# A transformer block on one core: another token order, other banks and tied products between output projection and up projection

## The chip, the core and the metric

The kernel runs on one core of one Trainium2 chip. The core has a matrix engine (TensorE, here PE, with its weight loads as PEld), a vector engine (DVE), a scalar engine (ACT), a general engine (POOL) and a queue that issues DMAs (SP). Each engine works through its own instructions in a fixed order and waits on semaphores for what the others deliver. [...] The metric is the device time of one execution in microseconds, lower is better.

## What is computed

One layer of a diffusion transformer: 1024 tokens of width 1024 on a 16 x 64 grid, 256 context tokens, 16 heads of 64 with a neighbourhood window of 8 x 16, and a gated feed-forward of width 2816.

```python
h  = modulate(rms_norm(x, norm1), sh1, sc1)        # sh, sc, g: adaLN of the condition c
hc = modulate(rms_norm(ctx, norm1), csh1, csc1)
q, k, v = heads(h @ w_q), heads(h @ w_k), heads(h @ w_v)     # q and k are RMS-normalised; kc, vc from hc
y  = neighbourhood_attention(q, k, v, kc, vc, rpb) @ w_o
x  = x + g1 * y
a, g = split(modulate(rms_norm(x, norm2), sh2, sc2) @ w_up)
out = x + g2 * ((a * gelu(dwconv3(g))) @ w_down)
```

All data are float32. The kernel multiplies in a faster reduced format (fp32r): each operand is split into a high part and a rest, and each product is three matmuls (high x high, high x rest, rest x high).

## The kernel before

The tokens are kept as eight tiles of 128 (NB = 8). The program runs in these stages:

1. adaLN of the attention branch and the first norm; tokens transposed and split.
2. Attention. For each of 8 pairs of heads the q, k and v projections (`qkv_gen`) are woven between the attention of the pair before. One step of attention (`stage_b`, `stage_c`, `stage_d`) handles one head and one tile of tokens: scores into the two banks with the tag "s", softmax on DVE, ACT and POOL, transposes of the probabilities through banks "tr" (three), the product with v into bank "po" (one). Two neighbouring tiles make a pair u, whose result goes to DRAM (`o_dram`, L456). In the last head the tiles come in the order LORD (L542).
3. Output projection (`wo_part`), in two halves over the heads. The first half (pairs of heads 0 to 3) runs beside the last heads' attention. The second half is the loop at L725: for each tile in the order TP it loads the heads' rows (L515), splits them (ACT L518, POOL L519), does 24 matmuls of 512 columns into two banks (L525 to L527) and adds them to the residual `x1[t]` (DVE L528). The banks are the two with tag "pq".
4. `h2_tile(t)` (L621): the residual goes to DRAM (L622); the second norm is a sum of squares on ACT (L155), a small DVE instruction (L156), a root on POOL (L157) and a scaling of all 1024 columns on DVE (L626). Eight PE transposes (L631) turn the tile, and four copies on DVE (L635) and four on ACT (L637) apply the modulation, writing back into `x1[t]`.
5. `combine(t)` (L695): the up projection uses seven products of half-size blocks in place of eight (Winograd's form). Its right-hand operands b1 to b7 are made of the token tiles: for a tile below 4 only b1 and b2 are split (ACT L646, then DVE L647, or POOL L647 for b3, b5 and b6); for tile 4 + m four sums with tile m (L710 to L713) and the splits of b3 to b7. Each of b1 and b2 is complete when tiles 0 to 3 are done; b3 to b7 need all eight. `combine` follows one tile late (LAG = 1).
6. Up projection. For each of 11 groups i of rows and its two parts (1 the gate, 0 the other factor) there are seven products in the order WORD, of 12 matmuls each (`up_mm`, L740). Part 1 sums in three banks "tr", part 0 in the two "pq" and in "po", and both use a half of "s" for the ops 7 and 4. The weights come by DMA (L667) into buffers `x1` that the token tiles have left; `raw_up` makes three sums of them (DVE L673 to L675) and `prep_up` splits an operand (ACT L687, POOL L688). The list `useq` sets the products' order in the program; operands are prepared up to six products ahead (UA = 6).
7. Convolution, gelu and gate of each group, and the down projection, also in seven products.

The program text gives a rank to each instruction. A planner then places them: it keeps a simulated clock for the engines and, when an engine is free, takes the ready instruction with the best rank, so the order on an engine can differ from the text. `tc.high_priority()` gives the instructions traced in its block a better rank. `tc.issue_after(ins)` adds an edge of order without a wait: what the block traces on the engine of `ins` is placed behind `ins` in that engine's queue. A buffer (`slot`, `xslot`, `ps.tile`) with a tag is given out again when the last reader of its former content is done.

Of the kernel before, what the change touches and what calls it, by code (L numbers as in the profile page):

```python
# [18 lines left out]
P = 128  # L19
# [23 lines left out]
TP = [0, 1, 4, 5, 2, 6, 3, 7]  # L43
LORD = [0, 1, 4, 5, 2, 3, 6, 7]
# [17 lines left out]
def block_kernel(ctx, tc, x, ctxt, cc, w_mod, b_col, b_row, n1, n2, w_qkv, gains, rpb_t, mask_i, mask_r, w_o,  # L62
# [96 lines left out]
    # adaLN of the attention branch, normalised and modulated tokens, transposed and split  # L159
# [112 lines left out]
    # attention, with the projections of the next pair of heads in between  # L272
# [185 lines left out]
    # adaLN of the rest, a little at a time  # L458
# [33 lines left out]
    # output projection: its first half runs beside the attention of the last heads  # L492
    xpool = ctx.enter_context(ExitStack())
    x1, wo, g1b, xsb = {}, [], [], []
# [18 lines left out]
    def wo_part(t, half):  # L513
# [6 lines left out]
        for hf in range(2):  # L520
            c = slice(hf * HALF, (hf + 1) * HALF)
            py = ps.tile([P, HALF], F32, tag="pq", bufs=2, name=f"py{half}_{t}_{hf}")
            for i in range(HP):
                wh, wl = wo[half * HP + i]
                PE.matmul(py, oh[:, i, :], wh[:, c], start=(i == 0), stop=False)  # L525
                PE.matmul(py, oh[:, i, :], wl[:, c], start=False, stop=False)  # L526
                PE.matmul(py, ol[:, i, :], wh[:, c], start=False, stop=(i == HP - 1))  # L527
# [14 lines left out]
    steps[-NB:] = [(NPAIR - 1, 1, t) for t in LORD]  # L542
# [62 lines left out]
    # rest of the output projection, second norm, operands of the Winograd form (seven products of halves  # L605
    # in place of eight) of the up projection: A is w_up^T in 2 x 2 blocks, B the tokens in 2 x 2 blocks
# [14 lines left out]
    def h2_tile(t):  # L621
# [4 lines left out]
        DVE.tensor_scalar(xn, x1[t], ss, None, ALU.mult)  # L626
        v = x1[t].rearrange("p (k n) -> p k n", n=P)
        for g in range(2):
            pt = ps.tile([P, 4, P], F32, tag="tr", bufs=3, name=f"pt2{t}_{g}")
            for k in range(4):  # L630
                PE.transpose(pt[:, k, :], xn[:, (4 * g + k) * P:(4 * g + k + 1) * P], ident)  # L631
# [17 lines left out]
    # up projection, gate with the token convolution; the gated rows and their sums go out for the down projection  # L649
# [4 lines left out]
    useq = [(0, 1, 1), (0, 1, 2), (0, 0, 1), (0, 0, 2)] + [(0, part, op) for part in (1, 0) for op in WORD[2:]]  # L654
# [23 lines left out]
    def prep_up(i, part, op):  # L678
        if (i, part) == (0, 1) and op in (1, 2):
# [15 lines left out]
    def combine(t):  # L695
# [3 lines left out]
        else:  # L699
# [18 lines left out]
            if t == 5:  # L718
                raw_up(0, 1)
                prep_up(0, 1, 1)  # L720
            if t == 6:
                prep_up(0, 1, 2)

    load_up(0, 0, 0)
    for n, t in enumerate(TP):  # L725
        wo_part(t, 1)
        vv[t] = h2_tile(t)
        if n >= LAG:
            combine(TP[n - LAG])
    for n in range(NB - LAG, NB):  # L730
        combine(TP[n])
# [82 lines left out]
    for k, (i, part, op) in enumerate(useq):  # L814
# [3 lines left out]
        if (i, part) not in gens:  # L818
            if part:
# [3 lines left out]
        next(gens[i, part])  # L823
# [156 lines left out]
```

## Time and profile before

| | |
|---|---|
| runs timed | 1492.29, 1489.33 and 1492.66 us |
| median of them | 1492.29 us |
| profiled execution, first to last instruction (span) | 1491.8 us |
| instructions | 22077 |
| mean granted clock of PE | 0.974 |
| PE busy | 1386.5 us |
| DVE busy | 1208.1 us |
| POOL busy | 805.7 us |
| ACT busy | 738.1 us |

The profiled execution is known by its span alone; it lies 0.5 us below the median of the timed runs. The profile's page has the busy time of each engine, a strip of 40 equal slices (each digit the busy share in tenths, PEclk the granted clock in tenths), and groups of instructions by line. The trace gives a timeline (start, duration, engine, line, operation, output <- inputs, shapes, how many merged, and in brackets the idle time before and what ended it), waits (who waited for whom: total, times, longest), and busy time by stretch. A line such as L740 is line 740 of the kernel before.

### The profile page before, as it was taken

The page shows a single profiled execution, that of the slowest core. Times are in us where ns is not written, and L with a number is a line of the kernel's source. Part 1 is how long each engine was busy: PE and PEld are TensorE (multiplying, and loading weights), DVE is VectorE, ACT ScalarE, POOL GpSimd, SP SyncE. Part 2 cuts the span into 40 slices and gives each one's busy share as a digit, 9 for nine tenths or more (in the row PEclk, how much of TensorE's full clock was granted, in tenths as well). Part 3 has the DMA queues.
Part 4 walks back from the last instruction along what each step waited for, and adds up shares of the span by engine and source line. Part 5 has one row for each costly group of instructions (what it writes and reads, how often), then busy time and mean ns, then how long its engine had stood idle before and what let it go on. Part 6 is the DMA issues. An engine that isn't in the chain of part 4 may idle for free.

```text
span 1491.8 us, 22077 instructions
## 1 busy us (share of the span) xinstructions
PE 1386.5 (93%) x7396; PEld 1200.0 (80%) x7396; DVE 1208.1 (81%) x2392; ACT 738.1 (49%) x1601; POOL 805.7 (54%) x672
## 2 busy tenths in 40 slices
PE   6689999999999999999996999999999987898998
PEld 2589889898989899888885777888888865686887
DVE  6778878888888878866589889788877779988884
ACT  6575645555565656645465434344343334244541
POOL 1455544545454546744368545555545568474872
PEclk9899999999999999999997999999999998899999
DMA  9612221313131202262132132233332347433343
GB/s 315 161 37 60 64 87 55 92 51 103 49 101 45 77 14 73 69 152 76 50 129 99 64 108 101 96 106 106 107 106 99 106 137 286 155 100 127 110 131 105
DMA packets 84827, 153.27 MB, mean 103 GB/s; under 512 B 9945, under 2 KB 49001, under 8 KB 84713
## 3 DMA queue, kind: packets, MB, share of 16 engines
q1 hardware_dynamic: 84712, 151.86, 32.7%
q8 instruction: 58, 0.95, 0.3%
q14 instruction: 57, 0.46, 0.1%
HBM read 119.05 MB, written 32.78 MB: 102 GB/s over the span
## 4 chain that ended last, share of the span: by engine, by line
PE 60%; DVE 20%; DMA 7%; POOL 5%; issue 4%; ACT 3%; SPq 0%; DVEq 0%; POOLq 0%; ACTq 0%
PE pg L740 8%; PE pa L740 7%; PE sw L740 6%; PE pq L301 5%; PE pq L303 5%; PE pq L305 5%; DMA mr<-in_w_mod_dram 2%; DVE y L787 2%; DVE p L410 2%; POOL u L688 2%; PE s L398 2%; PE po L448 2%; PE po L449 2%; PE py L525 2%; PE py L526 2%
## 5 line engine op out<-in xcount | busy, mean ns | idle before, releaser
L688 POOL TENSOR_TENSOR u<-ur,u 128x512 fp32r<-128x512 f32 x154 | 231.9, 1519 | 176.8 <-ACT u L687 175.1
L417 POOL TENSOR_TENSOR p<-p,m 128x640 f32<-128x640 f32 (+1 forms) x128 | 157.3, 1230 | 157.0 <-DVE m L413 116.0
L301 PE MATMUL pq<-wh,hth 128*128 128x384 f32 (+1 forms) x640 | 219.7, 343 | 17.1 <-DVE kn L340 15.3
L305 PE MATMUL pq<-wh,htl 128*128 128x384 f32 (+1 forms) x640 | 215.2, 336 | 2.4 <-DVE htl L194 1.4
L303 PE MATMUL pq<-wl,hth 128*128 128x384 f32 (+1 forms) x640 | 215.0, 336 | 0.5 <-POOL wl L147 0.5
L687 ACT ACTIVATE u<-ur 128x512 fp32r<-128x512 f32 x154 | 93.9, 628 | 116.1 <-PE sw L740 45.4
L412 ACT ACTIVATE p<-p,m 128x640 f32<-128x640 f32 (+1 forms) x128 | 102.9, 804 | 84.3 <-DVE m L410 75.2
L301 PEld LDWEIGHTS pq<-wh,hth 128*128 128x128 f32 x640 | 124.8, 195 | 23.1 <-DVE kn L340 9.2
L325 POOL TENSOR_TENSOR qss<-qss,mhalf 128x4 f32<-128x4 f32 (+1 forms) x80 | 79.9, 999 | 97.0 <-DVE qss L324 82.8
L305 PEld LDWEIGHTS pq<-wh,htl 128*128 128x128 f32 x640 | 124.7, 195 | 3.2 <-DVE htl L194 3.2
L303 PEld LDWEIGHTS pq<-wl,hth 128*128 128x128 f32 x640 | 124.8, 195 | 1.6 <-issue 0.9
L787 DVE SCALAR_TENSOR_TENSOR y<-g,cw,y 128x896 f32<-128x896 f32 (+1 forms) x132 | 102.8, 842 | 19.2 <-ACT y L781 19.1
L449 PE MATMUL po<-pt,v 128*128 128x256 f32 x352 | 93.3, 293 | 2.1 <-DVE pt L437 2.1
L448 PE MATMUL po<-pt,v 128*128 128x256 f32 x352 | 93.8, 289 | 0.1
L895 ACT ACTIVATE db<-dr 128x512 fp32r<-128x512 f32 x77 | 47.4, 629 | 87.3 <-PE dx L911 55.7
L871 POOL TENSOR_TENSOR da<-da 128x512 fp32r<-128x512 f32 x44 | 74.9, 1725 | 27.4 <-ACT da L870 27.4
L896 POOL TENSOR_TENSOR db<-dr,db 128x512 fp32r<-128x512 f32 x44 | 64.9, 1494 | 45.6 <-ACT db L895 34.3
L410 DVE CUSTOM_DVE_ANT_0 p<-s,bias 128x640 f32<-128x640 f32 x96 | 78.3, 816 | 9.5 <-PE s L399 8.9
L436 ACT ACTIVATE pt<-pl 128x384 fp32r<-128x384 f32 (+1 forms) x128 | 58.0, 461 | 47.6 <-PE pl L429 46.6
L471 DVE SCALAR_TENSOR_TENSOR macc<-mr,cs,macc 128x256 f32<-128x256 f32 x112 | 65.0, 581 | 13.9 <-DMA mr<-in_w_mod_dram 13.0
L437 DVE TENSOR_TENSOR pt<-pl,pt 128x384 fp32r<-128x384 f32 (+1 forms) x128 | 65.4, 516 | 6.7 <-ACT pt L436 6.2
L449 PEld LDWEIGHTS po<-pt,v 128*128 128x128 f32 x352 | 66.6, 189 | 4.0 <-DVE pt L437 3.4
(258 smaller groups left out, 4184.3 us busy)
## 6 DMA issues: line engine op xcount, KB each, us to landing
ur<-in_w_up_dram SPq DMA_DIRECT2D x44, 512.0 KB
da<-act_dram SPq DMA_DIRECT2D x77, 256.0 KB
mr<-in_w_mod_dram SPq DMA_DIRECT2D x128, 128.0 KB
dr<-in_w_down_dram SPq DMA_DIRECT2D x22, 512.0 KB
wraw<-in_w_qkv_dram SPq DMA_DIRECT2D x56, 192.0 KB
mraw<-in_w_mod_dram SPq DMA_DIRECT2D x16, 512.0 KB
act_dram<-sa SPq DMA_DIRECT2D x11, 512.0 KB
act_dram<-y SPq DMA_DIRECT2D x11, 512.0 KB
```

Source lines behind the costliest of these rows:

```text
L301: PE.matmul(pq[:, c0:], hth[t][:, k, :], wh[:, c0:], start=(k == 0), stop=False)
L303: PE.matmul(pq[:, c0:], hth[t][:, k, :], wl[:, c0:], start=False, stop=False)
L305: PE.matmul(pq[:, c0:], htl[t][:, k, :], wh[:, c0:], start=False, stop=(k == KC - 1))
L410: DVE.tensor_tensor_reduce(out=dst, in0=src, in1=bb, scale=1.0, scalar=3e38, op0=ALU.add, op1=ALU.min, accum_out=m[:, 0:1])
L412: ACT.activation(w[:, :n], w[:, :n], AF.Exp, bias=m[:, 0:1], scale=-1.0, accum_out=m[:, 1:2])
L417: POOL.tensor_tensor(w[:, :n], w[:, :n], m[:, 2:3].broadcast_to([P, n]), ALU.mult)
L448: PE.matmul(po, v, th[:, j].rearrange("p a b -> p (a b)"), start=(m == 0), stop=False)
L449: PE.matmul(po, v, tl[:, j].rearrange("p a b -> p (a b)"), start=False, stop=(m == len(blks) - 1))
L687: ACT.activation(s[:, 0], r[op], AF.Copy)
L688: POOL.tensor_tensor(s[:, 1], r[op], f(s[:, 0]), ALU.subtract)
L740: PE.matmul(bank, a, b, start=(start and k == 0 and n == 0), stop=(k == 3 and n == 2), skip_group_check=True)
L787: DVE.scalar_tensor_tensor(o, i, w, o, ALU.mult, ALU.add)
```

## The change

It touches the last head, the second half of the output projection, and the first products of the up projection.

- The last head's attention runs its tiles in natural order (LORD is gone), and the tiles of the output projection come in the order 0, 1, 2, 4, 3, 5, 6, 7 in place of 0, 1, 4, 5, 2, 6, 3, 7.
- The second half of the projection sums in one tile `sy` with the tag "s" (the two score banks) in place of two with the tag "pq".
- For the tiles 6 and 7 (DIAG) the norm's factor is no longer applied to the 1024 columns. A diagonal matrix `dg` is made of it (identity times the factor, 128 columns, DVE), and the eight transposes become eight plain fp32 products of `x1[t]`'s blocks with `dg`.
- `useq` begins with part 0's products 1 and 2, then part 1's; before, it was the other way round. Part 0's two operands are prepared in `combine(4)`, from a load issued before the loop, into two buffers `x1`; part 1's raw weights are loaded and summed in `combine(6)`, where before this was `combine(5)` with operands prepared in `combine(5)` and `combine(6)`.
- The first four up products are traced under `issue_after` the last matmul of the output projection.
- `h2_tile(7)` and the last `combine(7)` are traced under high priority.

Comments that the change strips are left out.

```diff
--- before.py
+++ after.py
@@ -40,8 +40,8 @@
 WB = 21
 FT = -1
 WS = 512
-TP = [0, 1, 4, 5, 2, 6, 3, 7]
-LORD = [0, 1, 4, 5, 2, 3, 6, 7]
+TP = [0, 1, 2, 4, 3, 5, 6, 7]
+DIAG = (6, 7)
 GROUPS = [2, 3, 3, 3]
 LA, LB = 3, 2
 DA, DB = (2, 1, 7), (2, 1, 7)
@@ -489,9 +489,9 @@
                         DVE.scalar_tensor_tensor(dst, dst, 1.0, n2c[:, nk * hf:nk * (hf + 1)], ALU.add, ALU.mult)
                 yield
 
     xpool = ctx.enter_context(ExitStack())
-    x1, wo, g1b, xsb = {}, [], [], []
+    x1, wo, g1b, xsb, sy, last_wo = {}, [], [], [], [], []
     HP = NPAIR // 2
 
     def wo_prep(p):
@@ -519,12 +519,12 @@
         (POOL if half else DVE).tensor_tensor(ol, raw, f(oh), ALU.subtract)
         for hf in range(2):
             c = slice(hf * HALF, (hf + 1) * HALF)
-            py = ps.tile([P, HALF], F32, tag="pq", bufs=2, name=f"py{half}_{t}_{hf}")
+            py = sy[0][:, hf] if half else ps.tile([P, HALF], F32, tag="pq", bufs=2, name=f"py{half}_{t}_{hf}")
             for i in range(HP):
                 wh, wl = wo[half * HP + i]
                 PE.matmul(py, oh[:, i, :], wh[:, c], start=(i == 0), stop=False)
                 PE.matmul(py, oh[:, i, :], wl[:, c], start=False, stop=False)
-                PE.matmul(py, ol[:, i, :], wh[:, c], start=False, stop=(i == HP - 1))
+                last_wo[:] = [PE.matmul(py, ol[:, i, :], wh[:, c], start=False, stop=(i == HP - 1))]
             DVE.tensor_tensor(x1[t][:, c], py, x1[t][:, c], ALU.add)
 
     def wo_first():
@@ -539,7 +539,6 @@
             yield 20
 
     steps = [(p, h, t) for p in range(NPAIR) for h in range(2) for t in range(NB)]
-    steps[-NB:] = [(NPAIR - 1, 1, t) for t in LORD]
     useq_ = {}
     for p, h, t in steps:
         useq_.setdefault((p, h, t // 2), len(useq_) % 2)
@@ -623,12 +622,22 @@
         xn = slot("wx", f"xn{t}", F32)
         ss = const.tile([P, 1], F32, tag="ss", bufs=3, name=f"ss2{t}")
         norm_rows(x1[t], xn, ss)
-        DVE.tensor_scalar(xn, x1[t], ss, None, ALU.mult)
+        if t in DIAG:
+            src, dg = x1[t], usb.tile([P, P], F32, tag="dg", bufs=2, name=f"dg{t}")
+            DVE.tensor_scalar(dg, ident, ss, None, ALU.mult)
+        else:
+            src, dg = xn, None
+            DVE.tensor_scalar(xn, x1[t], ss, None, ALU.mult)
         v = x1[t].rearrange("p (k n) -> p k n", n=P)
         for g in range(2):
             pt = ps.tile([P, 4, P], F32, tag="tr", bufs=3, name=f"pt2{t}_{g}")
             for k in range(4):
-                PE.transpose(pt[:, k, :], xn[:, (4 * g + k) * P:(4 * g + k + 1) * P], ident)
+                c = slice((4 * g + k) * P, (4 * g + k + 1) * P)
+                if dg is None:
+                    PE.transpose(pt[:, k, :], src[:, c], ident)
+                else:
+                    PE.matmul(pt[:, k, :], src[:, c], dg, start=True, stop=True)
             for k in range(4):
                 kk = 4 * g + k
                 if g == 0:
@@ -646,12 +655,12 @@
             ACT.activation(h, r, AF.Copy)
             (POOL if op in HP_ else DVE).tensor_tensor(l, r, f(h), ALU.subtract)
 
     NP2 = NF // 2
     lo_, hi_ = slice(0, HALF), slice(HALF, SEQ)
     uraw, uop = {}, {}
     parts = [(i, part) for i in range(NP2) for part in (1, 0)]
-    useq = [(0, 1, 1), (0, 1, 2), (0, 0, 1), (0, 0, 2)] + [(0, part, op) for part in (1, 0) for op in WORD[2:]]
+    useq = [(0, 0, 1), (0, 0, 2), (0, 1, 1), (0, 1, 2)] + [(0, part, op) for part in (1, 0) for op in WORD[2:]]
     useq += [(i, part, op) for i, part in parts[2:] for op in WORD]
     cnt = [0]
 
@@ -676,7 +685,7 @@
         uraw[i, part] = {1: a11, 2: a12, 6: t2, 5: t1, 7: a21, 3: a12, 4: a22}
 
     def prep_up(i, part, op):
-        if (i, part) == (0, 1) and op in (1, 2):
+        if (i, part) == (0, 0) and op in (1, 2):
             s = xslot(f"u{i}_{part}_{op}", F32R)
         else:
             s = slot(("rh", "rl")[cnt[0] % 2], f"u{i}_{part}_{op}", shape=(P, 2, HALF))
@@ -715,20 +724,27 @@
             split_b(5, m, t1)
             split_b(6, m, t2)
             split_b(4, m, t4)
-            if t == 5:
+            if t == 4:
+                uraw[0, 0] = {op: load_up(0, 0, 0)[:, op - 1] for op in (1, 2)}
+                prep_up(0, 0, 1)
+                prep_up(0, 0, 2)
+            if t == 6:
                 raw_up(0, 1)
-                prep_up(0, 1, 1)
-            if t == 6:
-                prep_up(0, 1, 2)
 
     load_up(0, 0, 0)
+    sy.append(ps.tile([P, 2, HALF], F32, tag="s", bufs=1, name="sy"))
     for n, t in enumerate(TP):
         wo_part(t, 1)
-        vv[t] = h2_tile(t)
+        if t == TP[-1]:
+            with tc.high_priority():
+                vv[t] = h2_tile(t)
+        else:
+            vv[t] = h2_tile(t)
         if n >= LAG:
             combine(TP[n - LAG])
-    for n in range(NB - LAG, NB):
-        combine(TP[n])
+    with tc.high_priority():
+        for n in range(NB - LAG, NB):
+            combine(TP[n])
     raw_up(0, 0)
     tmp00 = xslot("tmp0_0")
 
@@ -816,11 +832,15 @@
             prep_up(*useq[nprep])
             nprep += 1
         if (i, part) not in gens:
-            if part:
+            if i not in g:
                 g[i] = [slot("wx", f"g{i}_{m}", F32) for m in range(2)]
                 y[i] = [slot("t4", f"y{i}_{m}", F32) for m in range(2)]
             gens[i, part] = up_part(i, part, g[i] if part else y[i])
-        next(gens[i, part])
+        if k < 4:
+            with tc.issue_after(last_wo[0].ins):
+                next(gens[i, part])
+        else:
+            next(gens[i, part])
         if op == WORD[-1]:
             if part:
                 for m in range(2):
```

## The prediction

> **What bounds the kernel now.** I read the page first, then busy time by stretch around the changed place, then what TensorE (PE) waited for there.
>
> ```profile
> span 1491.8 us, 22077 instructions
> PE 1386.5 (93%) x7396; PEld 1200.0 (80%) x7396; DVE 1208.1 (81%) x2392; ACT 738.1 (49%) x1601; POOL 805.7 (54%) x672
> PE   6689999999999999999996999999999987898998
> PEclk9899999999999999999997999999999998899999
> ```
>
> PE is busy 93% of the span, and the two strips have a hole in common: near the middle PE falls to 6 and the granted clock to 7. That slice is the passage from the output projection to the up projection, where all of the change lies.
>
> ```profile
> 731.50:786.60 55.10, 53.58 (x271) 44.36 (x271) 39.74 (x78) 33.34 (x84) 31.90 (x32) 1.00 0.37 123
> 786.60:827.00 40.40, 27.39 (x93) 20.87 (x94) 38.02 (x50) 20.83 (x51) 34.46 (x28) 0.75 0.24 78
> 860.00:1230.00 370.00, 364.96 (x1563) 292.70 (x1562) 304.77 (x356) 145.21 (x224) 197.24 (x131) 1.00 0.32 108
> ```
>
> The columns are length, then busy time of PE, PEld, DVE, ACT, POOL, the clock, the DMA share and GB/s. The projection's second half (first row) is PE-bound with DVE idle for 15.4 us. In the passage (second row) PE is idle for 40.40 - 27.39 = 13.0 us at a mean clock of 0.75, and DVE works 38.02 of 40.40 us: there DVE is the bound. The up projection (third row) is PE-bound again (364.96 of 370), so time won in the passage reaches the end.
>
> ```profile
> PE pt L631 <- DVE xn L626: 5.5, 2, 5.3
> PE pg L740 <- ACT b3h L646: 2.9, 1, 2.9
> PE sw L740 <- DVE b7l L647: 2.4, 1, 2.4
> PE pa L740 <- ACT b1h L646: 1.9, 1, 1.9
> PE py L525 <- DVE x L528: 1.2, 1, 1.2
> ```
>
> These are PE's waits from 722 to 840 us (total, times, longest). The longest of L631 (5.3) and the row of pa with b1h are both tile 3, last but one in the old order: the up products 1 and 2 need all of tiles 0 to 3, so none could start before tile 3 was normalised, transposed and split. The rows with b3h and b7l are tile 7's: its transposes held the banks, then its sums were late.
>
> ```profile
> 786.20 0.39 PE L527 MATMUL py<-woh,ohl 128*128 128x512 f32 x1
> 791.90 1.94 PE L631 MATMUL pt<-ident,xn 128*128 128x128 f32 x8 [5.32 <-DVE xn L626]
> 795.74 0.79 PE L740 MATMUL pa<-b1h,u 128*128 128x512 f32 x1 [1.90 <-ACT b1h L646]
> 794.31 0.14 DVE L156 TENSOR_SCALAR ss<-ss 128x1 f32<-128x1 f32 x1
> 795.45 5.52 POOL L688 TENSOR_TENSOR u<-ur,u 128x512 fp32r<-128x512 f32 x4
> 800.94 0.73 POOL L157 TENSOR_TENSOR ss<-ss,mhalf 128x1 f32<-128x1 f32 x1
> 801.70 1.77 DVE L626 TENSOR_SCALAR xn<-x,ss 128x1024 f32<-128x1024 f32 x1 [0.44 <-POOL ss L157]
> ```
>
> The last projection matmul starts at 786.20; the first up product runs at 795.74. Tile 7's root (L157) could have run after 794.45 and ran at 800.94, behind weight splits (L688) queued in front of it on POOL.
>
> **What is lost there.** Two windows of the up matmuls alone (L740; PE, PEld, clock, DMA share, GB/s), and one tile's eight transposes:
>
> ```profile
> 780.00:827.00 47.00, 24.82 (x77) 18.40 (x78) 0.78 0.23 79
> 827.00:840.00 13.00, 13.00 (x57) 10.52 (x56) 1.00 0.25 82
> 746.34 1.03 PE L631 MATMUL pt<-ident,xn 128*128 128x128 f32 x8
> ```
>
> At full pace a matmul takes 13.00 / 57 = 0.228 us. By 827 there were 77, worth 17.6 us, and 16 transposes, worth 2 x 1.03: 19.7 us of work in 40.4 us. So 20.7 us are lost, 13.0 idle and 7.7 to the slow clock. That is nearly all that the change can win.
>
> **The change, part by part.** *Token order 0, 1, 2, 4, 3, 5, 6, 7, with the last head in natural order.* Tile 3 moves from behind the end of the projection to the fifth place. Its eight transposes (1.03 us) go ahead on PE, and these DVE rows leave the passage:
>
> ```profile
> 790.00 1.76 DVE L626 TENSOR_SCALAR xn<-x,ss 128x1024 f32<-128x1024 f32 x1
> 793.03 1.37 DVE L635 TENSOR_SCALAR x<-pt,s,b 128x128 f32<-128x128 f32 x4 [0.67 <-PE pt L631]
> 795.72 2.69 DVE L647 TENSOR_TENSOR b1l<-x,b1h 128x256 fp32r<-128x256 f32 x2 [1.27 <-ACT b1h L646]
> 798.34 2.92 DVE L647 TENSOR_TENSOR b2l<-x,b2h 128x256 fp32r<-128x256 f32 x2
> 757.16 0.75 DVE L647 TENSOR_TENSOR b1l<-x,b1h 128x256 fp32r<-128x256 f32 x2
> ```
>
> Together 1.76 + 1.37 + 2.69 + 2.92 = 8.7 us. Earlier, where POOL is mostly idle, the same pair of splits took 0.75 (last row), so ahead they cost some 3.6 us, inside DVE's 15.4 idle. In exchange the heavy combines (tiles 4, 5) come one and two places later: that is a rival below. The heads' own order moves no work; the second half still needs the score banks read, and its last pair of tokens is still done last.
>
> *Score banks.* The second half's sums go to the two banks of the scores, two halves in turn as before with two buffers: cost nothing. It frees the banks of the up product's part 0, so that part 0's products 1 and 2 can be first. Their weights are split in the middle of the projection into freed x1 buffers: two POOL splits (1.65 us each in the passage, by the mean of the row below) leave it.
>
> ```profile
> L688 POOL TENSOR_TENSOR u<-ur,u 128x512 fp32r<-128x512 f32 x12 | 19.6, 1652 | 0.9 <-ACT u L687 0.5
> L675 DVE TENSOR_TENSOR ur<-ur,ur 128x512 f32<-128x512 f32 x3 | 2.6, 863 | 0.0
> ```
>
> *Four products tied behind the last matmul.* 4 x 12 x 0.228 = 10.9 us of PE work that needs only tiles 0 to 3. The tie itself is an order in PE's queue, no wait; queued behind it are only up products, which before ran later anyway.
>
> What this must cover is tile 7's chain. In an undisturbed tile the way from the projection's add to the end of the scaling is 752.90 to 756.38, 3.5 us:
>
> ```profile
> 752.90 0.69 DVE L528 TENSOR_TENSOR x<-py,x 128x512 f32<-128x512 f32 x1 [0.39 <-PE py L527]
> 755.63 0.75 DVE L626 TENSOR_SCALAR xn<-x,ss 128x1024 f32<-128x1024 f32 x1 [0.66 <-POOL ss L157]
> ```
>
> With some 2 us of transposes, 1.4 of copies out, an add and a split of op 5 (about 0.7 each on DVE and ACT, 1.65 on POOL) it is 10 to 11 us: just covered. If that cover is gone, PE stands idle as it does now.
>
> *Diagonal form for tiles 6 and 7.* The scaling of 1024 columns (0.75 undisturbed, 1.77 in the passage) becomes a 128-column one. No such row exists; its bounds are 0.14 (L156, one column) and 0.40 (L635, 128 columns out of PSUM). I take 0.3, saving 1.5 us a tile in the passage. PE multiplies in plain fp32 instead of transposing. The nearest fp32 product with a 128x128 stationary is L485, two calls, four records:
>
> ```profile
> 232.67 0.53 PEld L485 LDWEIGHTS pmc<-ones,macc 128*128 128x128 f32 x4
> ```
>
> The starts are (0.53 - 0.19) / 3 = 0.11 us apart (0.19: one load), two records a call, so eight calls take 16 x 0.11 to 0.12 = 1.9 us against 1.03. If they cost the same as transposes the extra is 0; if a record cost a full load of 0.19, 3.0 us and 2.0 extra. I take 0.9 extra for each tile.
>
> *Priority.* It moves tile 7's instructions ahead of weight splits on POOL, ACT, DVE and SP wherever the planner finds them ready. Worth up to 800.94 - 794.45 = 6.5 us, already within the 20.7. Tile 7's store of 512 KB (L622) moves too: SP stands at it until L528 ends, 0.7 us behind the projection, and the loads of weights queue behind it. The copies out overwrite the stored rows and wait for it: 3 to 4 us (256 KB took 2.95, quoted below) beside the chain's 3.5 and the 1.9 of products, so hidden; 1 us if it isn't.
>
> **The sum.** PE first. The projection ends at 786.6 - 1.2 (the wait for L528, bounds 0 and 1.2) + 1.0 (tile 3) + 0.9 (tile 6) = 787.3. From there 17.6 + 1.9 = 19.5 us without a stall: the state of 827 would be reached at 806.8, a gain of 20.2. Now DVE, the bound of the passage: 38.0 - 8.7 - 1.5 = 27.8 us of its work remain behind 787.3, which ends at 815.1, a gain of 11.9. But one of the three sets of L673 to L675 in that stretch is for the next part of weights (3 x 0.68 = 2.0), which PE doesn't need yet: 813.1, a gain of 13.9. I take this: PE won't run before DVE feeds it. Span 1491.8 - 13.9 = 1477.9; the runs' median lies 0.5 above the span, so 1478.4. Its own range is a gain of 9 to 20, 1472 to 1483.
>
> A short stall costs more than itself:
>
> ```profile
> 811.78 0.47 PE L740 MATMUL pg<-b2h,u 128*128 128x512 f32 x1 [2.93 <-ACT b3h L646]
> 811.80:816.40 4.60, 4.60 (x13) 0.63 0.64 216
> ```
>
> After 2.93 us of waiting the clock was 0.63 over 4.6 us, so 1.7 us more; the 6.3 us left between the two sums hold one such stall (4.6).
> [...]
>
> **Rivals.** *Weights of part 1 late (gain 4 to 9).* Part 0 now takes the x1 buffers that freed first, so part 1's loads wait for the combines of 5 and 6.
>
> ```profile
> 775.24 1.02 SPq L667 DMA_DIRECT2D ur<-in_w_up_dram  x2
> 808.10 8.94 SPq L667 DMA_DIRECT2D ur<-in_w_up_dram  x5
> 727.89 2.95 DMA oraw<-o_dram
> 782.59 1.85 POOL L647 TENSOR_TENSOR b6l<-x,b6h 128x256 fp32r<-128x256 f32 x2
> ```
>
> They went at 775.24; now at best after tile 5's last split (784.4 in the old order). With 3 to 4 us of landing (256 KB took 2.95), an ACT copy of 0.6 and a POOL split of 1.65 the operand is there at 791, before 787.3 + 5.5 + 1.9 = 794.7, when PE wants it. If the third buffer or the splits come 6 us later, PE waits 6 and slows for 1.7 to 3.4: of 13.9 remain 4 to 8; 1484 to 1488. For it: POOL's share in the passage, 34.46 of 40.40. Against: two more buffers free with the first two products.
>
> *The same, much later (gain near 0).* If the loads go at 808, as the second pair's did, the third product starts near 814, and 53 matmuls (12.1 us) at a clock first halved end at 828: 1491 to 1494.
>
> *Slower: the priority holds the queues.* DVE, ACT and POOL run in order. If the planner thinks tile 7's chain is ready earlier than it is, its instructions stand at the head of DVE while ready work waits behind. The price is DVE's idle time behind the projection's end: up to the whole chain, 11 us, and 5 more for the combine of tile 7 that hangs on it. DVE's 27.8 + 16 = 43.8 would end at 831, 4 later than before; 1492 to 1497. It decides from 40.4 + 786.6 - 787.3 - 27.8 = 11.9 us of such idle time. Against: now DVE idles only 2.4 us in that passage with the planner's own order.
>
> *The tie doesn't act so.* If tile 6's or 7's products stand in PE's order before the four, PE waits out the 3.5 us and half rate: 5 to 7 of the gain, 1483 to 1486; counted with the first rival.
>
> **Chances.** Forecast 0.60, more than 20 won 0.04, first and last rival 0.18, loads at 808 0.08, slower 0.10. A measurement of this kernel tells some 0.2% (3 us) from nothing, so faster 0.82, same 0.08, slower 0.10. The range holds the forecast and the partial gains: 1471 to 1489.
>
> **What would show it.** Right: four products start within 0.5 us of the last L527 and run some 11 us at full clock; no L631 wait above 2 us; DVE rows of tile 3 before the end of the projection; L157 of tile 7 within 1.5 us of its L156; DVE near 28 us from there to the 77th up matmul. Wrong: a PE gap over 3 us before the first product of part 1, loads of L667 behind 795, DVE idle above 8 us, or a projection that ends after 790.

## The result, and the profile after

The change makes the kernel slower: 1504.31 us, the median of four runs (1503.1 to 1504.95), against 1490.81 us, the median of four runs of the kernel before. The ratio is 1.0084, with a 95% interval of 1.0066 to 1.0102. Forecast was 1478.4. The profiled execution took 1503.1 us, with a span of 1501.3.

The page of the kernel after, its head and the two strips that were read before:

```profile
span 1501.3 us, 22103 instructions
PE 1386.5 (92%) x7412; PEld 1197.9 (80%) x7412; DVE 1215.6 (81%) x2392; ACT 739.9 (49%) x1601; POOL 802.0 (53%) x672
PE   6699999999999999989986999999999998798998
PEclk9899999999999999999998999999999999899999
```

PE is busy for the same 1386.5 us as before, so the longer span is idle time of PE. The hole in the middle is still there, at the same place and a little less deep at the clock (8 instead of 7).

The same stretches as before, in the kernel after: from the first matmul of the projection's second half to its end, from there to the 77th up matmul, and the up projection (length, busy PE, PEld, DVE, ACT, POOL, clock, DMA share, GB/s):

```profile
727.90:795.30 67.40, 60.01 (x288) 47.24 (x289) 41.81 (x89) 37.26 (x92) 30.64 (x31) 0.97 0.25 86
795.30:833.90 38.60, 23.63 (x94) 18.19 (x93) 37.18 (x38) 18.27 (x45) 36.99 (x31) 0.82 0.31 109
860.00:1230.00 370.00, 363.67 (x1552) 292.02 (x1551) 312.63 (x357) 145.27 (x221) 203.64 (x134) 0.99 0.30 104
```

The projection takes 67.4 us where it took 55.1, and PE idles 7.4 us of them (67.40 - 60.01; before 1.5). The passage takes 38.6 us where it took 40.4; 25.8 were forecast. DVE works 37.18 and POOL 36.99 of the 38.60 us, so between them these two fill the passage; before it was 38.02 and 34.46 of 40.40.

What PE waited for from 722 to 840 us in the kernel after:

```profile
PE sw L756 <- DVE b7l L656: 8.1, 1, 8.1
PE sy L525 <- DVE x L528: 6.4, 6, 2.0
PE pg L756 <- ACT x L646: 2.8, 1, 2.8
PE pa L756 <- ACT u L696: 2.2, 1, 2.2
```

The wait for tile 3's scaling (5.3 before) and that for b1h are gone. Two rows stand in their place: the longest wait is now for the low part of b7 (b7l), and the projection waits for its own copies out, L528, six times.

To compare all runs stage by stage, the times below count from the last score read-out of the attention, L410. Its rows in the kernel before and in the kernel after (shortest, median and longest in ns, first and last start):

```profile
L410 DVE DVE_READ_ACCUMULATOR2_ANT m<- x4: 83/84/85, 723.9 to 730.6; 128x1 f32 x4
```

```profile
L410 DVE DVE_READ_ACCUMULATOR2_ANT m<- x3: 82/82/83, 723.5 to 727.1; 128x1 f32 x3
```

So zero is 730.6 us in the one and 727.1 in the other. All kernels do the same work up to there, the last head's tiles in one of two orders. In the fourteen profiles zero lies between 724.9 and 731.1 us, with either order, so a difference there is not put down to an edit. One profiled execution stands for each kernel; the sums' distances from the 761.2 of the kernel before agree with those of the medians within 3 us. Marks are read off the timeline: the end of the last projection matmul, the start of the 77th and of the 1500th up matmul, the first down matmul, the end.

```
                   to the end of   to the    to the     to the first   to the   sum
                   the projection  77th up   1500th up  down matmul    end
before                  55.9         40.5      333.1        82.1        249.6   761.2
after                   68.2         38.6      334.8        82.6        250.0   774.2
e1_before_sy            73.3         31.0      334.7        83.0        248.9   770.9
e2_after_pq             56.0         43.7      335.3        87.9        250.4   773.3
e3_after_two            56.4         46.2      334.0        85.9        251.3   773.8
e4_after_order          69.0         32.6      335.2        87.6        249.5   773.9
e5_pq_order             58.3         39.9      335.8        83.1        250.5   767.6
e6_pq_nopri             55.9         43.8      335.5        85.9        250.5   771.6
e7_pq_nodiag            56.1         41.2      335.0        83.0        249.0   764.3
e8_pq_poolrelief        54.7         38.7      335.6        83.9        248.8   761.7
e9_pq_order_nodiag      58.4         37.6      335.2        81.3        250.2   762.7
e10_pq_order_nodiag_act 58.2         34.4      334.7        82.6        250.6   760.5
e11_before_diag         55.8         40.0      331.1        83.3        250.1   760.3
e12_pq_notie            55.8         43.9      335.2        87.7        249.0   771.6
```

The kernel after loses 12.3 us in the projection, wins 1.9 in the passage, and loses 1.7 by the 1500th up matmul and 0.9 behind it: 13.0. So the question is two questions: why did the projection become longer, and why did the passage not become shorter?

### The profile page after: what moved, and what is told of

It reads as the page before. It is cut to its first block, busy times and chain, and to the rows that moved or that the text cites. A ratio compares the mean times of both kernels' runs of the same rounds, so it can differ in the third digit from the quotient of the medians.

```text
span 1501.3 us, 22103 instructions
## 1 busy us (share of the span) xinstructions
PE 1386.5 (92%) x7412; PEld 1197.9 (80%) x7412; DVE 1215.6 (81%) x2392; ACT 739.9 (49%) x1601; POOL 802.0 (53%) x672
## 4 chain that ended last, share of the span: by engine, by line
PE 64%; DVE 18%; DMA 7%; issue 4%; ACT 3%; POOL 3%; SPq 1%; DVEq 0%; POOLq 0%; ACTq 0%
PE pg L756 8%; PE pa L756 8%; PE sw L756 6%; PE pq L301 5%; PE pq L303 5%; PE pq L305 5%; DMA mr<-in_w_mod_dram 2%; PE s L398 2%; PE dtr L929 2%; PE po L448 2%; PE po L449 2%; PE pl L429 2%; PE dtr L930 2%; PE dtr L931 2%; DVE y L803 1%
## 5 line engine op out<-in xcount | busy, mean ns | idle before, releaser
L325 POOL TENSOR_TENSOR qss<-qss,mhalf 128x4 f32<-128x4 f32 (+1 forms) x80 | 80.2, 1003 | 95.5 <-DVE qss L324 81.3
L803 DVE SCALAR_TENSOR_TENSOR y<-g,cw,y 128x112 f32<-128x112 f32 (+1 forms) x132 | 109.6, 897 | 21.4 <-ACT y L797 21.4
L891 POOL TENSOR_TENSOR da<-da 128x512 fp32r<-128x512 f32 x44 | 67.7, 1562 | 38.9 <-ACT da L890 38.9
L410 DVE CUSTOM_DVE_ANT_0 p<-s,bias 128x640 f32<-128x640 f32 x96 | 78.2, 815 | 9.0 <-PE s L399 8.2
L890 ACT ACTIVATE da<-da 128x512 fp32r<-128x512 f32 x77 | 47.9, 630 | 47.1 <-DMA da<-act_dram 46.1
```

What stands on the lines that cost most here:

```text
L325: POOL.tensor_tensor(ss[:, 4 - n:], ss[:, 4 - n:], mhalf[:, 4 - n:], ALU.pow)
L803: DVE.scalar_tensor_tensor(o, i, w, o, ALU.mult, ALU.add)
```

## The experiments

### First question: the projection

Theory: the two halves of the tile `sy` don't take turns as two buffers do; each half's first matmul waits for the copy out of the other half. Rivals: the new order of the tiles, or the diagonal products among the projection's matmuls. Two changes from the first half of a tile to its second in the kernel after (timeline; in brackets the idle time and what ended it):

```profile
745.12 0.39 PE L527 MATMUL sy<-woh,ohl 128*128 128x512 f32 x1
745.55 0.69 DVE L528 TENSOR_TENSOR x<-sy,x 128x512 f32<-128x512 f32 x1
746.39 0.47 PE L525 MATMUL sy<-woh,ohl 128*128 128x512 f32 x1 [0.88 <-DVE x L528]
...
771.64 1.76 DVE L720 TENSOR_TENSOR x<-x,x 128x512 f32<-128x512 f32 x1 [0.65 <-POOL x L719]
772.38 0.39 PE L527 MATMUL sy<-woh,ohl 128*128 128x512 f32 x1
773.33 0.74 DVE L656 TENSOR_TENSOR b7l<-x,b7h 128x256 fp32r<-128x256 f32 x2
774.00 0.68 DVE L528 TENSOR_TENSOR x<-sy,x 128x512 f32<-128x512 f32 x1
774.73 0.50 PE L525 MATMUL sy<-woh,ohl 128*128 128x512 f32 x1 [1.97 <-DVE x L528]
775.41 0.63 PE L527 MATMUL sy<-woh,ohl 128*128 128x512 f32 x1
775.83 0.63 PE L525 MATMUL sy<-woh,ohl 128*128 128x512 f32 x1
...
778.39 0.49 PE L525 MATMUL sy<-woh,ohl 128*128 128x512 f32 x1
```

The last matmul of one half ends at 745.51, DVE copies it out at once, and only then the next half's first matmul runs, though it writes another bank: 0.88 us of idle PE. In the second place DVE is busy with a combine (L720, L656) when the half is ready at 772.77, so the copy comes 1.2 us late and PE idles 1.97. Behind that gap eight matmuls start 0.43 us apart ((778.39 - 775.41) / 7) instead of 0.23. Between two tiles the change is covered by a tile's transposes (eight took 1.06 us at 749.64 us, and the next first matmul ran at 750.46 without a wait).

**e1_before_sy: only the sums in one tile.** The kernel before with this alone:

```diff
+    sy.append(ps.tile([P, 2, HALF], F32, tag="s", bufs=1, name="sy"))
...
-            py = ps.tile([P, HALF], F32, tag="pq", bufs=2, name=f"py{half}_{t}_{hf}")
+            py = sy[0][:, hf] if half else ps.tile([P, HALF], F32, tag="pq", bufs=2, name=f"py{half}_{t}_{hf}")
```

> The kernel before with one edit: the projection's second half sums in the two halves of one tile in the score banks; order, products and priority as before. Theory A (the two halves are waited for as one buffer: each half's first matmul waits for the copy-out of the other half): PE waits 6 to 8 us on L528 in that stage and the whole is 7 to 12 us slower than before, 1498 to 1503. Rival B (the waits come from a DVE that is late because the heavy combines moved; the banks cost nothing): no such waits, 1489 to 1493.

**e2_after_pq: the kernel after with the sums back in two tiles.** The same line the other way round.

> The changed kernel with the second half's sums back in two tiles of the old banks; everything else of the change stays. Theory A: the waits on L528 fall from 6.4 to below 2 us, the projection ends 8 to 12 us earlier after its first matmul, total 1493 to 1498. Rival B: the waits stay, total 1502 to 1506.

**e3_after_two: the first half in the score banks, the second in a "pq" tile.**

```diff
-            py = sy[0][:, hf] if half else ps.tile(...)
+            py = sy[0][:, hf] if half and hf == 0 else ps.tile(...)
```

> The changed kernel with only the first half of each token tile in the score banks and the second half in a tile of the old banks, so two halves are two tiles. Theory A: as with both in the old banks, 1493 to 1498. A third reading (the score banks themselves are slow to come free or to be read) would leave waits on every second half: 1498 to 1502. Rival B: 1502 to 1506.

**e4_after_order: the kernel after with the old order of tiles** in the projection and in the last head.

```diff
-TP = [0, 1, 2, 4, 3, 5, 6, 7]
+TP = [0, 1, 4, 5, 2, 6, 3, 7]
+LORD = [0, 1, 4, 5, 2, 3, 6, 7]
```

> The changed kernel with the token order and the last head's order of before; banks, tied products, diagonal form and priority as changed. Theory A: the waits on the one tile stay, about 6 us, and tile 3 is late again, so 1500 to 1508. Rival B (the late heavy combines are the cost): near before, 1489 to 1496.

Measured: e1 1503.05 us, ratio 1.0075 (1.0047 to 1.0103); e2 1503.43, 1.0085 (1.0057 to 1.0114); e3 1504.55, 1.0085 (1.0057 to 1.0113); e4 1505.99, 1.0098 (1.0063 to 1.0132). What PE waited for in e1 from 720 to 840 us:

```profile
PE sy L525 <- DVE x L528: 11.2, 7, 5.3
PE pt L631 <- DVE xn L626: 7.6, 3, 6.8
```

The one line of e1 brings the wait into the kernel before (11.2 us for L528, where 6 to 8 were expected) and lengthens its projection from 55.9 to 73.3. Two tiles instead of one, in e2 as in e3, where one of them even lies in a score bank, bring the kernel after back to 56.0 and 56.4. With the old order (e4) it stays at 69.0. So it is the one tile, not the banks and not the order, and the first theory holds for the projection. The trace puts the wait down to DVE's L528; no run tells whether the banks themselves would have needed it, or only the program's bookkeeping of the tile.

The times of e2 and e3 are another matter: 1493 to 1498 was expected, and they came out at 1503.43 and 1504.55, where the rival had them. e2 is no faster than the kernel after: the 12 us come back from the projection and are lost again behind it, 5.1 of them in the passage (38.6 to 43.7) and 5.3 on the way from the 1500th up matmul to the first down matmul.

### Second question: the passage

The passage of e2, in the same columns, and the first sums of the heavy combines on DVE in e2, and then in the kernel after:

```profile
782.50:826.20 43.70, 27.79 (x110) 20.94 (x109) 40.77 (x45) 21.81 (x54) 41.14 (x35) 0.77 0.32 109
785.87 0.69 DVE L720 TENSOR_TENSOR x<-x,x 128x512 f32<-128x512 f32 x1 [1.03 <-POOL x L719]
795.62 1.23 DVE L720 TENSOR_TENSOR w<-x,x 128x512 f32<-128x512 f32 x1
802.41 1.21 DVE L720 TENSOR_TENSOR x<-x,x 128x512 f32<-128x512 f32 x1
```

```profile
801.40 0.68 DVE L720 TENSOR_TENSOR x<-x,x 128x512 f32<-128x512 f32 x1
811.85 1.22 DVE L720 TENSOR_TENSOR w<-x,x 128x512 f32<-128x512 f32 x1
```

In e2 DVE and POOL both work for 41 of 43.7 us. Of the four heavy combines (tiles 4 to 7) three begin behind the end of the projection at 782.5; in the kernel after it is two, behind 795.3: its longer projection gave DVE and POOL time to start one more. That fits the 5.1 us that e2 loses in the passage; the 5.3 us before the first down matmul it doesn't explain.

Theory: the passage is bound by DVE and POOL, which carry the heavy combines and the weights at once. Rivals: the priority puts things in a bad order; the diagonal form costs more than its price; the tie doesn't cover tile 7. All four runs start from e2.

**e5_pq_order: the heavy tiles earlier.**

```diff
-TP = [0, 1, 2, 4, 3, 5, 6, 7]
+TP = [0, 1, 4, 5, 2, 3, 6, 7]
+LORD = [0, 1, 4, 5, 2, 3, 6, 7]
```

> The run with the old banks, and the tokens in the order 0, 1, 4, 5, 2, 3, 6, 7 (the last head as before): the heavy combines of 4 and 5 go early again, tile 3 still ends before the projection does. Theory C (the passage is long because the combines of 5, 6 and 7 all fall behind the projection's end): from the last scores to the 77th up matmul 84 to 90 us in place of 99.7, total 1486 to 1494. Rival D (sharing between DVE and POOL makes the same work take as long in any order): 96 to 100, total 1500 to 1504.

**e6_pq_nopri: without both priorities.**

```diff
-            with tc.high_priority():
-                vv[t] = h2_tile(t)
+            vv[t] = h2_tile(t)
...
-    with tc.high_priority():
-        for n in range(NB - LAG, NB):
-            combine(TP[n])
+    for n in range(NB - LAG, NB):
+        combine(TP[n])
```

> The run with the old banks, without both priorities. If the priority puts tile 7's combine ahead of tile 6's, which is needed as much: to the 77th up matmul 94 to 98 us in place of 99.7, 2 to 5 us faster. If the priority helps as meant: 102 to 106, slower by 2 to 6. If the planner's order is much the same: within 1.5.

**e7_pq_nodiag: tiles 6 and 7 scaled and transposed as before.**

```diff
-DIAG = (6, 7)
+DIAG = ()
```

> The run with the old banks, with the old scaling and transposes for tiles 6 and 7. If the diagonal form saves 1.5 us of DVE for each tile as predicted: to the 77th up matmul 102 to 103 us in place of 99.7. If its DVE instruction is stretched as much and its products hold PE: 98 to 100.

**e8_pq_poolrelief: less for POOL.** The subtraction that makes the low part of the first group's weights is left out; a copy on ACT fills the same buffer, and the products that use it stay.

```diff
-        POOL.tensor_tensor(s[:, 1], r[op], f(s[:, 0]), ALU.subtract)
+        if i == 0:
+            ACT.activation(s[:, 1], r[op], AF.Copy)
+        else:
+            POOL.tensor_tensor(s[:, 1], r[op], f(s[:, 0]), ALU.subtract)
```

> The run with the old banks; for the first group's 14 weight operands POOL doesn't subtract: the low part is a second copy of the full value on ACT, so the low part of these products is left out (replaced by another value). It takes about 21 us of POOL work out of the passage. Theory (POOL and DVE stretch each other and bound the passage together): DVE's 512-column sums fall from 1.2 to 1.75 us towards 0.68, to the 77th up matmul 80 to 87 us in place of 99.7. Rival (the combines' own order and chain bound it, whatever POOL does): 94 to 99.

Measured: e5 1496.39 us, ratio 1.0042 (1.0024 to 1.0059); e6 1504.98, 1.0094 (1.0072 to 1.0116); e7 1493.42, 1.0007 (0.9992 to 1.0021); e8 1492.67, 1.0015 (0.9997 to 1.0033). In the passage of e2, the work on the raw weights alone (tile `ur`; their sums on DVE, copies on ACT, subtractions on POOL, in this order); then in e8 the whole passage and the same part:

```profile
782.50:826.20 43.70, 14.46 (x11) 6.72 (x11) 17.25 (x12) 0.77 0.32 109
```

```profile
783.40:822.10 38.70, 24.84 (x109) 19.09 (x108) 30.55 (x48) 26.99 (x67) 26.99 (x23) 0.82 0.35 115
783.40:822.10 38.70, 11.79 (x14) 12.53 (x22) 0.00 (x0) 0.82 0.35 115
```

The priority changes nothing in the passage (43.8 against 43.7). The earlier heavy tiles take 3.8 us off the passage but add 2.3 to the projection. POOL's relief takes 5.0 us off the passage: DVE, whose own instructions were left alone, is busy 30.55 us instead of 40.77, and the weights' sums take 0.84 us each (11.79 / 14) instead of 1.31 (14.46 / 11). So POOL's work makes DVE's longer, and the theory holds in kind. In size it falls short: less than a third of POOL's 17.25 us comes back. PE's longest waits in e8 are for b7 (7.5 us for b7l, 5.2 for b7h), and no engine there is busy for more than 30.55 of the 38.70 us; this speaks for the rival, that the combines' own order and chain bound it. Without the diagonal form the passage is 2.5 us shorter.

The expectations named the 77th up matmul, 99.7 us behind zero in e2. It came at 98.2 in e5, where the rival had it (96 to 100) and not the theory (84 to 90); at 99.7 in e6, as for an order that stays the same; at 97.3 in e7, earlier than both expectations had it (98 to 100 and 102 to 103); and at 93.4 in e8, between the theory's 80 to 87 and the rival's 94 to 99 and nearer the rival's.

In e5, e7 and e8 much of the gain in time lies elsewhere: e7 is 10.0 us faster than e2, of which 4.9 arise between the 1500th up matmul and the first down matmul; of the 10.8 of e8 it is 4.0. The last runs were to tell whether the diagonal form does that.

### The last runs

**e9_pq_order_nodiag: e5 and e7 together.**

> The changed kernel with the sums back in the two old buffers, the heavier tiles 4 and 5 third and fourth (tokens 0, 1, 4, 5, 2, 3, 6, 7, the last head in the same order) and tiles 6 and 7 scaled and transposed as before. Alone, on the two old buffers, the order gave 7.0 us and the old scaling 10.0, of which only 1.5 and 2.4 lay in the passage (to the 77th up product) and the rest at the hand-off to the down projection. If the two are independent: 77th product 96 us after the last score copy, time 1486. If most of both is the same shift of the hand-off (first down product 83 us behind the 1500th up product in both): 77th at 96, time 1490 to 1493, no change against the kernel before.

**e10_pq_order_nodiag_act: e9, and ACT scales tiles 6 and 7.**

```diff
-            DVE.tensor_scalar(xn, x1[t], ss, None, ALU.mult)
+            if t in (6, 7):
+                ACT.activation(xn, x1[t], AF.Copy, scale=ss)
+            else:
+                DVE.tensor_scalar(xn, x1[t], ss, None, ALU.mult)
```

> The run before this one with one edit more: ACT instead of DVE scales the rows of tiles 6 and 7 (two operations of 128x1024, about 1.06 us on ACT by its squares, 1.49 on DVE in the passage). If DVE and POOL together bound the passage, 3.0 us less for DVE bring the 77th product 2 to 4 us forward and the time as much. If POOL alone bounds it, or ACT's own queue, nothing: within 1 us.

**e11_before_diag: the kernel before with its last two tiles, 3 and 7, in the diagonal form.**

```diff
+DIAG = (3, 7)
...
+        if t in DIAG:
+            src, dg = x1[t], usb.tile([P, P], F32, tag="dg", bufs=2, name=f"dg{t}")
+            DVE.tensor_scalar(dg, ident, ss, None, ALU.mult)
...
+                    PE.matmul(pt[:, k, :], src[:, c], dg, start=True, stop=True)
```

> The kernel before with one edit: its last two tiles, 3 and 7, in the diagonal form. If the diagonal form costs 10 us by itself (as its removal gave in the kernel with two old buffers): 1501. If only its direct price counts (2 x 0.9 us of PE against 2 x 1.2 us of DVE saved) and the rest was the planner's order at the hand-off to the down projection: 1489 to 1494, and the distance from the 1500th up product to the first down product of 82 to 86 us moves with no relation to it.

**e12_pq_notie: e2 without the tie.**

```diff
-        if k < 4:
-            with tc.issue_after(last_wo[0].ins):
-                next(gens[i, part])
-        else:
-            next(gens[i, part])
+        next(gens[i, part])
```

> The changed kernel on the two old buffers without the tie of the four up products behind the last projection matmul. If the tie does what the prediction took (covers tile 7's chain with 10.9 us of products): without it the first product starts 5 to 10 us behind the last projection matmul, at a slower clock, the 24th up product comes 6 to 10 us later than 71.3, and the time is 1503 plus 0 to 8. If the planner places the four there anyway: 71.3 and 1503 again. If DVE and POOL alone bound the passage: the 24th later, but the 77th at 99.7 all the same.

Measured, against 1490.46 us for the kernel before: e9 1493.37 us, ratio 1.0021 (1.0003 to 1.0038); e10 1491.02, 1.0002 (0.9984 to 1.0020); e11 1489.01, 1.0005 (0.9985 to 1.0025); e12 1503.61, 1.0090 (1.0057 to 1.0122). The ratios are those of the record and not quotients of the two medians: e11's median is the lower one, its ratio 1.0005. The end of the projection in e12, and the passages of e9 and of e10:

```profile
784.08 0.39 PE L527 MATMUL py<-woh,ohl 128*128 128x512 f32 x1
784.31 0.40 PE L755 MATMUL pa<-b1h,u 128*128 128x512 f32 x1
```

```profile
784.60:822.20 37.60, 24.68 (x94) 17.69 (x94) 36.81 (x44) 19.19 (x47) 32.03 (x26) 0.81 0.29 98
```

```profile
785.90:820.30 34.40, 24.67 (x94) 18.52 (x93) 31.83 (x39) 20.78 (x49) 31.78 (x26) 0.80 0.32 107
```

The tie changes nothing: without it the first up matmul also follows the projection at once (784.31 behind 784.08), and every stage is that of e2 within 0.2 us but the last, which is 1.4 shorter. (The 71.3 us that the expectation gives to the 24th up matmul of e2 are its 48th, the last of the four products; in e12 that one comes at 71.2.) The diagonal form alone costs the kernel before nothing that can be told (e11), so the 10 us of e7 aren't its price by itself; what else they hang on was not shown. Order and scaling together (e9) give the smaller of the two expected gains: 1493.37, with the 77th up matmul at 96.0. ACT's scaling takes 3.2 us off the passage, as the bound by DVE and POOL had it, for 5.0 us less of DVE; of these 3.2 about 2 reach the end (762.7 to 760.5), and the two runs' intervals overlap. No version is shown to be faster than the kernel before.

**What stays open.** The stretch from the 1500th up matmul to the first down matmul takes 81.3 to 83.9 us in nine kernels and 85.9 to 87.9 in five (e2, e3, e4, e6, e12). No edit changes the program's text there. The five all have tiles 6 and 7 in the diagonal form, but so have the kernel after, e5 and e8. Whether it is the planner's placing there was not tried. For the kernel after itself it matters little: there the stretch is 82.6 against 82.1.

## Why the prediction was wrong

It forecast a span of 1477.9; the span is 1501.3, so 23.4 us are to be accounted for. The last score came 3.5 us earlier than in the profile before, which lies within the spread of zero above. From there the projection was to take 55.9 + 0.7 = 56.6 us and took 68.2 (+11.6); the passage was to take 25.8 and took 38.6 (+12.8); the rest lost 1.7 and 0.9. Sum: -3.5 + 11.6 + 12.8 + 2.6 = 23.5. (The 0.5 us that the forecast puts between span and time is too little, as the profiled execution of the kernel after shows: 1503.1 us with a span of 1501.3. It is no part of this sum.)

**The step that failed first: "Score banks ... two halves in turn as before with two buffers: cost nothing".** One tile of two banks was not waited for as two buffers here: its price is 12 us in the kernel after and 17 in e1. The profile before did hold a bound for it: L528 takes 0.69 us there, so eight uncovered changes of half, one in each tile, are at least 5.5 us. In the kernel after the undisturbed change at 745 us cost 746.39 - 745.12 - 0.23 = 1.04 us, and eight such are 8.3; copies that come late, as at 774 us, and half pace behind them (0.43 us a matmul instead of 0.23) come on top. The prediction put this edit at nothing and gave no price for the case that two halves are not two buffers.

**The second: "38.0 - 8.7 - 1.5 = 27.8 us of its work remain", less 2.0.** Tile 3's rows did leave the passage, but DVE still worked 37.18 us. e2 shows that this step fails by itself: there the projection ends in time and all four tied products run behind it, and the passage still takes 43.7 us. The work of L647 (before) and L656 (after) on DVE and POOL, and that on the weights (`ur`; DVE, ACT, POOL), first before, then after:

```profile
786.60:827.00 40.40, 12.19 (x14) 11.25 (x12) 0.75 0.24 78
786.60:827.00 40.40, 9.21 (x10) 7.12 (x12) 19.64 (x12) 0.75 0.24 78
```

```profile
795.30:833.90 38.60, 12.92 (x12) 15.06 (x16) 0.82 0.31 109
795.30:833.90 38.60, 13.26 (x11) 6.71 (x11) 17.61 (x11) 0.82 0.31 109
```

Before, tile 3's four splits took 2.69 + 2.92 of the 12.19, so the ten of b4 and b7 took 6.6 us, 0.66 each. After there are twelve and they take 12.92, 1.08 each: 6.3 more. The weights' sums take 4.1 more, one instruction more and 1.21 each instead of 0.92. With smaller terms on both sides that is the 9.4 us from 27.8 to 37.2; the 2.0 that were to be left for later didn't leave either. Two things were missing from the sum. "The heavy combines (tiles 4, 5) come one and two places later: that is a rival below" was said, but the rivals below priced it as late loads and as waiting, not as more work in the passage: there are two more splits on DVE and four more on POOL (16 for 12, 15.06 us for 11.25), from tile 5. The larger part is the other: every duration was taken as it stood in the profile before. Of the 6.3 us for the splits two more at 0.66 are 1.3, and longer durations 5.0. So DVE was not the one bound that the sum took it for: POOL, for which no sum was made, worked 36.99 of the 38.60 us, and DVE's durations hang on what POOL does.

**POOL's share.** In the kernel after, DVE's instructions by form from 727.9 to 833.9 us (shortest, median, longest in ns; first and last start):

```profile
L644 DVE TENSOR_SCALAR x<-pt,s,b x32: 393/402/412, 742.3 to 807.6; 128x128 f32<-128x128 f32 x32
L528 DVE TENSOR_TENSOR x<-sy,x x16: 676/690/693, 733.5 to 797.0; 128x512 f32<-128x512 f32 x16
L722 DVE TENSOR_TENSOR x<-x x3: 674/1217/1777, 775.7 to 810.2; 128x512 f32<-128x512 f32 x3
L656 DVE TENSOR_TENSOR b4l<-x,b4h x6: 411/950/1478, 777.4 to 819.5; 128x256 fp32r<-128x256 f32 x6
```

L528 and L722 have the same shape and the same shortest time; L528 reads one operand out of PSUM (a bank that PE wrote) and never takes longer than 0.69 us, and L644, which reads PSUM too, stays within 0.02 us; L722 reads both operands from SBUF and takes up to 2.6 times as long. The weights' sums of the profile before, both operands in SBUF, show the same two lengths, 1.23 us with POOL at work (2.86 of the 3.00 us from 816.00) and 0.68 with POOL idle (0.00 of the 5.55 us from 823.05):

```profile
816.08 1.23 DVE L674 TENSOR_TENSOR ur<-ur,ur 128x512 f32<-128x512 f32 x1
817.24 1.23 DVE L675 TENSOR_TENSOR ur<-ur,ur 128x512 f32<-128x512 f32 x1
818.06 3.23 POOL L688 TENSOR_TENSOR u<-ur,u 128x512 fp32r<-128x512 f32 x2
...
825.31 0.68 DVE L674 TENSOR_TENSOR ur<-ur,ur 128x512 f32<-128x512 f32 x1
825.91 0.68 DVE L675 TENSOR_TENSOR ur<-ur,ur 128x512 f32<-128x512 f32 x1
...
828.62 4.24 POOL L688 TENSOR_TENSOR u<-ur,u 128x512 fp32r<-128x512 f32 x3 [5.58 <-ACT u L687]
```

And in e8, with less work on POOL, DVE's busy time falls from 40.77 to 30.55 us. POOL was at work beside all three L722 of the kernel after, that of 0.67 us at 797.63 too, so which of POOL's instructions lengthen which of DVE's was not shown.

**What held.** The first up products did start right behind the last projection matmul, at full pace (clock 1.00 from 795.29 to 801.06), here in the kernel after:

```profile
789.81 0.29 DVE L628 TENSOR_SCALAR dg<-ident,ss 128x128 f32<-128x128 f32 x1 [0.66 <-POOL ss L157]
...
795.06 0.39 PE L527 MATMUL sy<-woh,ohl 128*128 128x512 f32 x1
795.29 0.40 PE L756 MATMUL pa<-b1h,u 128*128 128x512 f32 x1
...
798.92 0.15 DVE L156 TENSOR_SCALAR ss<-ss 128x1 f32<-128x1 f32 x1 [0.62 <-ACT xn L155]
800.66 0.40 PE L756 MATMUL pa<-b2h,u 128*128 128x512 f32 x1
800.83 0.72 POOL L157 TENSOR_TENSOR ss<-ss,mhalf 128x1 f32<-128x1 f32 x1
802.01 0.74 DVE L628 TENSOR_SCALAR dg<-ident,ss 128x128 f32<-128x128 f32 x1
802.85 2.02 PE L640 MATMUL pt<-dg,x 128*128 128x128 f32 x16 [1.79 <-issue]
804.63 0.48 PE L756 MATMUL pg<-b1h,u 128*128 128x512 f32 x1
```

But only two of the four cover tile 7: 24 matmuls to 801.06. Its diagonal products stand in PE's order before the third, and PE idles 1.8 us. The profile names no releaser ("issue"), but dg is done at 802.75, 0.1 us before they start, and dg stood behind tile 6's sum (L720) on DVE, the root behind tile 6's combine on POOL. That is the rival "the tie doesn't act so" in small. Two matmuls of the third product follow, and then the first of the fourth waits 2.8 us for a copy out of the banks (the row with L646 above): part 1 sums in the banks that tile 7's transposes had used, which the sum didn't price. The sixteen records took 2.02 us where 1.9 were taken: 0.25 us a plain fp32 product of 128 columns, where an fp32r matmul of 512 columns takes 0.23. dg cost 0.74 us where 0.3 was taken (its bounds were 0.14 and 0.40), though 0.29 for tile 6, inside the projection. The root stood 1.76 us behind L156, not 1.5 and not 6.5. The one wait for L528, 1.2 us, that the sum took off came back as six, 6.4 us together. With two tiles (e2) the projection ends at 56.0, near the forecast 56.6.

**The rivals.** Weights of part 1 late: PE shows no wait of part 1 for its weights (the 2.2 us for u are of `pa`, part 0), so this is no main cause. The 1.7 to 3.4 us that its price held for the slow clock were the author's estimate; measured are 1.7 us behind the wait of 8.12 us for b7l in the kernel after (0.70 over the 5.62 us from 826.38) and 3.3 us in the profile before (0.50 over the 6.60 us from 795.74). Priority holding the queues, the one that ended on the slower side: it was given 10%, and in e6, built on e2, leaving the priority out has no effect. So the time ended on that side by another mechanism, one that no rival named. Of the signs that were to show the forecast wrong, "a projection that ends after 790" came true: it ended at 795.3. So did "loads of L667 behind 795": they start at 798.32, right behind tile 7's store, as the prediction had them queue; ACT waited 0.8 us for what they brought. Of the signs for right, DVE's 28 us and four products in a row failed.

## What to carry to other kernels

Two halves of one PSUM tile were waited for as one buffer here: when a sum moves from two tiles into halves of one, price each change of half with the copy out plus what may stand before it in the copying engine's queue (PE idled 0.79 to 1.97 us at each of six changes in the kernel after). When work is moved off a passage, list what takes its old place there, and take durations on DVE from rows with POOL as busy as it will be: in the profile before, the weights' sum L674 took 0.68 us with POOL idle and 1.23 with POOL at work. And undo each part of a bundle alone: here removing the loss in the projection (e2) left the time where it was, because the passage grew by 5.1 us and a later stretch, for a reason not found, by 5.3.

## What the runs showed of the hardware

Behind a gap of 1.97 us PE ran at half pace: eight matmuls 0.43 us apart, at a granted clock of 0.50 from 775.4 to 778.4 us, where the projection around them runs at 0.23. In the profile before it ran at half pace, too, behind 2.93 us (a clock of 0.50 from 813 to 816 us). The length alone doesn't decide: in the kernel after, behind 2.28 us (at 601.60) and 2.60 us (at 869.18), the clock stayed at 1.00, up to 611.00 and 874.00.

POOL's work cost DVE time here without a wait that the profile names: 17.25 us less on POOL for the weights (e8; POOL's busy time in the passage fell from 41.14 to 26.99) went with 10.2 us less of DVE's busy time, 40.77 to 30.55, for 45 and 48 instructions.
